# Layer 0's output projection in sixteen-tile block products, with on-chip shift columns, a ScalarE rotary exchange and another cut of the last two chunks

## The chip, the cores and the metric

One core of a Trainium2 chip runs the whole kernel. The metric is the time of one execution on the device in microseconds (us). The kernel before was timed three times: median 2083.02 us, from 2081.39 to 2084.38. A separate execution was taken with the profiler; every duration below is from that one.

## What is computed

A two-layer backbone works on 640 columns of activations: 128 context tokens and 512 latent tokens, 2048 features each. Cut to what matters here:

```
for l in (0, 1):
    h = rms_norm(x) * (1 + scale) + shift          # shift, scale, gate from silu(c) @ ada_w[l]
    q, k, v, ..., gp = split(h @ w_in[l])
    y = concat(branch_1, branch_2) * silu(gp)       # l = 0: window attention with rotary | GLA
                                                    # l = 1: neighbourhood attention | gMLP
    x = x + gate * (y @ w_out[l])                   # the output projection
out = rms_norm(x) * final_norm_g
```

The rotary embedding of layer 0 multiplies q and k by a cosine table and adds their 32-row blocks, exchanged in pairs (0 with 1, 2 with 3), times a sine table. Ten such steps run, for two k heads and eight q heads.

## The kernel before

All matrix products are fp32 in accuracy and are made of three TensorE products of two-part numbers: an activation is `acth + actl`, a weight is `whi + wlo`, and one product of a 128x128 weight tile costs three matmuls (high x high, high x low, low x high). Activations lie with features on the partitions, 16 k-tiles of 128 features, 640 columns in two halves of 320. `mm_k` and the inner function `three` of `spair` issue these matmuls (L396 is the helper `mm`).

**Weights.** A raw tile group of four k-tiles (128x512) is loaded from DRAM by SyncE, ScalarE copies it to `whi` (a rounding copy), and GpSimd or VectorE subtracts to `wlo`. `wpump` does this ahead of the matmuls, into a ring `whl` of 2560 columns, so at most five such units are live. The program is written by a planner in Python: it keeps a model of each engine's clock (class `Pace`), and tasks that yield (`spawn`, `tick`) issue their instructions between matmuls where that model says that there is room. Engines run their instructions in the order of issue, SyncE its DMAs too.

**Pairs of chunks.** An output chunk is 128 output features. Most chunks are computed two at a time as a 2x2 block product after Strassen and Winograd (`spair`): the blocks are the two chunks, the k-tiles 0 to 7 and 8 to 15, and the two column halves; seven block products stand in place of eight. Each product runs over four k-tiles per unit. The products named S1, S2 and A22 take sums of activations. For k-tiles 0 to 3 these sums stay on chip in `eh` and `el` (the near tiles); for k-tiles 4 to 7 (the far tiles) they lie in the DRAM tensor `far_dram` and are loaded to four slots of the pool `tail`, one load per slot and product, by `far_load`, each time after the product that last read the slot. S3 takes sums from `t3_dram`, which replace the second column half of `acth` and `actl` for k-tiles 0 to 7 while pairs run; `fold` makes all this, `unfold` brings the saved second half back from `bh_dram` and `bl_dram`. A pair can also be short (`ns == NR`): then only k-tiles 0 to 3 and 8 to 11 go through block products, the other eight are done plainly, and no far sums are needed. A full pair is 7 x 8 x 3 = 168 matmuls, a short one 7 x 4 x 3 + 2 x 8 x 2 x 3 = 180, two plain chunks 192.

**The output projections.** Each has 16 chunks: 0 and 1 as a plain pair (`kpair`), 2 to 13 as six pairs, 14 and 15 plain. `SHORT = 6, 2` says how many of the six are short: all six in layer 0, the first two in layer 1. In layer 0, chunks 14 and 15 are a `kpair` during which the next layer's activations are formed as tiles come free (`to_odd`: ScalarE writes `acth`, VectorE `actl`); while that runs, the shift columns of layer 1 (two columns per k-tile, `fs` for the far tiles) are computed and one DMA writes them to `far_dram`, whose rows have 2 + 320 columns. Then the plain pair of layer 1's first two chunks starts. VectorE also computes the adaLN vectors of the coming layers from `ada` rows in the background (custom instructions on `adas`).

**The last two chunks** (`hpair`, L955 on) end the program: half 0 of chunk 14, half 0 of chunk 15, then half 1 of each, so that the final norm of half 0 (`final(0)`) runs under half 1. Each half takes its own weight split: `unit(c, k, r)` for r = 0 and 1, sixteen units in all. After half 0, `prescale` multiplies five tiles (`POOLED`) of half 1 by the norm weight on ScalarE so that GpSimd can finish them. `final(1)` stands alone at the end: sum of squares, a product with ones, five steps to the reciprocal root, then a scaling of each of 16 tiles and 8 stores.

**Rotary** (`rope`): four DMAs of 32 rows each exchange the blocks of q within SBUF into `sw`, then VectorE multiplies and adds.

Of the kernel before, what the change touches and what calls it, by code (L numbers as in the profile page):

```python
# [32 lines left out]
NR = 4  # L33
CW = 2 + HT
RING = 2560
WINDOWS = ((0, 2), (2, 2), (4, 4), (8, 4))
# [7 lines left out]
GHOSTS = 12, 13  # L44
SHORT = 6, 2

# [189 lines left out]
class Trunk:  # L236
# [378 lines left out]
    def wstart(self, chunks, acts):  # L615
        self.chunks = chunks
        self.jobs, self.plain = [], []
        self.job, self.nraw, self.nsplit = 0, 0, 0
        self.parts, self.live, self.wpat = {}, {}, 0
        self.su, self.su_free = None, 0  # L620
        self.wfree_at = 0.0

        self.gates = []
        J = self.jobs

        def unit(c, k, r=0):
            gate, slot = self.gates.pop(0) if self.gates else (0, self.plain[-1][2] + 1 if self.plain else 0)
            J.append(("split", (c, k, r), slot % 4, 4, chunks[c][1]))
            self.plain.append((c, k, slot, gate))

        for k in (0, 4, 8, 12):
            for c in range(FIRST):
                unit(c, k)
        self.both = {c for kind, x in acts if kind == "h" for c in x[:2]}
        work = [x for x in acts if x[0] != "f"]
        for n, (kind, x) in enumerate(work):
            if kind == "c" and x >= FIRST:
                for k in (0, 4, 8, 12):
                    unit(x, k)
            elif kind == "k":  # L640
                seen = set()
                for c, k in self.skew(*x[:3]):
                    if (c, k - k % 4) not in seen:
                        seen.add((c, k - k % 4))
                        unit(c, k - k % 4)
            elif kind == "h":
                for r in range(2):
                    for c in x[:2]:
                        for k in (0, 4, 8, 12):
                            unit(c, k, r)  # L650
# [122 lines left out]
    def wpump(self, force=False):  # L773
# [47 lines left out]
        else:  # L821
            a = self.space(n * M)
            if a is None:
                return False
            hl = [x[:, a : a + n * M].rearrange("p (a b) -> p a b", b=M) for x in self.whl]
        outs = [] if lead else [pc.span(hl[0])]
# [5 lines left out]
        else:  # L832
            self.live[key] = (a, a + n * M)
            self.wpat = a + n * M
        hi, lo = hl
# [27 lines left out]
    def wdone(self, key):  # L863

        del self.parts[key]
        if key in self.live:
            del self.live[key]
        else:
            self.su_free += 1
# [12 lines left out]
    def mm_k(self, c, k, outs, first=0, last=KT - 1, r=0):  # L882
# [4 lines left out]
        for p, half in outs:  # L887
            cs = self.cols(half, shift)
            h, l = self.ah[:, k, cs], self.al[:, k, cs]
# [37 lines left out]
    def kpair(self, c1, c2, order, ready=None, free=None):  # L927
# [25 lines left out]
        self.quiet = False  # L953

    def hpair(self, c1, c2, after):  # L955

        for half in range(2):
            if half:
                self.need("unfold0", "unfold1")
                self.quiet, self.hold = True, 6.0  # L960
            for c in (c1, c2):
                if half == 0 and self.chunks[c][3]:
                    self.chunks[c][3]()
                p = self.pj()
                for k in range(KT):
                    self.mm_k(c, k, [(p, half)], r=half)
                    self.kdone(c, k, half)
                    if k % 2:
                        self.tick(1 + 2 * half)
                self.chunks[c][4](*((p, None) if half == 0 else (None, p)))  # L970
                self.drop(p)
# [217 lines left out]
    def fold(self, ready, used, far_used, shift=None, yt=None):  # L1189
# [59 lines left out]
        def shifts():  # L1249
# [4 lines left out]
            for f, x, scale in ((0, a, -1.0), (1, a, 1.0), (2, u, 1.0)):  # L1254
                self.split2(self.eh[:, :, f, 0:2], self.el[:, :, f, 0:2], x[:, :NR], scale)
                self.split2(fs[:, :, f, 0, :], fs[:, :, f, 1, :], x[:, NR:], scale)
                yield
            e = self.far.rearrange("p i f a b -> p (i f a) b")[:, :, 0:2]
            self.dma(e.bitcast(U32), self.fs.bitcast(U32))
            self.flags.add("shifts")  # L1260

        def far(w):
# [26 lines left out]
            for i in range(NR + w, NS, 2):  # L1289
                yield from self.wait(f"{ready}:{i}", f"{ready}:{NS + i}")  # L1290
                (j1, j2), (m1, m2) = [(x[:, one], x[:, two]) for x in (yt(i), yt(NS + i))]
                keep(i)
                out = lambda f: self.far[:, i - NR, f, :, 2:]
                yield from sub(j1, j2, j1)
# [844 lines left out]
    def out_evac(self, l, f, xsrc, spill):  # L2139
        nc = self.nc  # L2140
        box = {}
        at = HT

        def square(y, c):
            if l == 1 and f == KT - 1:
                nc.scalar.activation(self.sq, y[:, c], AF.Square)
            else:
# [190 lines left out]
    def program(self):  # L2338
# [5 lines left out]
        self.hsp = tc.nc.dram_tensor(HSP, [128, 6, T], F32, kind="Internal").ap()  # L2344
        self.far = tc.nc.dram_tensor(FAR, [128, NS - NR, 3, 2, CW], F32R, kind="Internal").ap()
        self.t3 = tc.nc.dram_tensor(T3D, [128, NS, 2, HT], F32R, kind="Internal").ap()
# [477 lines left out]
    def open_gate(self):  # L2824
# [3 lines left out]
        self.ssq, last = self.take(), self.take(1024)  # L2828
        self.last, self.sq = last, last[:, :HT]
        self.wsT, self.gb = (last[:, 512 * i : 512 * i + 512].rearrange("p (a b) -> p a b", b=128) for i in range(2))  # L2830
        L["ms"] = [self.xr.list[0][:, :HT], self.xr.list[1][:, :HT]]

    POOLED = (2, 5, 8, 11, 13)

    def prescale(self):
        c = slice(HT, T)
        for k in self.POOLED:
# [3 lines left out]
            yield  # L2841
        self.flags.add("prescaled")
        yield

    def final(self, half):
        nc, d, Y, L = self.nc, self.d, self.Y, self.L
        c = slice(HT, T) if half else slice(0, HT)
        n = c.stop - c.start
        x, t = (m[:, :n] for m in L["ms"])
        if half:  # L2850
            yield from self.wait("fr", "prescaled")
# [4 lines left out]
        yield from self.until(self.sq)  # L2856
        self.mm(p[:, :n], self.ones, self.sq, start=False)
        if not half:
# [4 lines left out]
        q = self.sm()[:, :n]  # L2863
        self.rsqrt(r, x, t, q)
        if half:
            nc.scalar.activation(r, q, AF.Copy)
            self.flush()
        else:
            self.flags.add("fr")
            self.spawn(self.prescale())  # L2870
            yield
        for k in range(KT):
# [3 lines left out]
            elif k % 2:  # L2876
                two = Y[:, k - 1 : k + 1, c]
            if half and k in self.POOLED:
                nc.gpsimd.tensor_tensor(y, y, r, ALU.mult)
# [184 lines left out]
```

## Time and profile before

| | |
|---|---|
| median of three runs | 2083.02 us (2081.39 to 2084.38) |
| the profiled execution's own time | 2079.31 us |
| its span, first to last instruction | 2077.5 us |
| TensorE busy | 2026.5 us, 98% |
| VectorE, GpSimd, ScalarE busy | 73%, 53%, 46% |
| mean granted TensorE clock | 0.994 of full speed |
| moved by DMA | 412.52 MB, mean 199 GB/s |

How to read it: matmuls overlap, so a matmul's own duration (some 310 ns) is longer than the step from one to the next, and a busy TensorE says only that something was in its pipe. The stages lie in the span as follows, by the loads of their weights: layer 0's output projection from about 845 to 1050 us, layer 1's from about 1850 to the end, the last two chunks from 2027.6 us.

### The profile page before, as it was taken

Reading aid. Unit: us, or ns where it says so; the run is one execution under the profiler, and the core shown is the slowest. Engines: PE = TensorE matmul, PEld = TensorE weight load, DVE = VectorE, ACT = ScalarE, POOL = GpSimd, SP = SyncE. Lnnn points to the kernel's source line nnn. Section 1 sums busy time; section 2 is a strip of 40 time slices with the busy share of each in tenths; the row PEclk is TensorE's granted clock in tenths of the full one; section 3 lists DMA queues with packets and bytes.
Section 4 is the critical chain, followed back from the end, with each engine's and each line's share of the span. In section 5 each row is a group of like instructions: output and inputs, shape, how many; then the busy total and the mean of one; then the engine's idle time right before and its main releaser. Section 6 shows DMA issues by size and latency. Waiting matters only on the chain. (4 is left out here: it accounts for less than half of the span.)

```text
span 2077.5 us, 38922 instructions
## 1 busy us (share of the span) xinstructions
PE 2026.5 (98%) x13930; PEld 1965.5 (95%) x13930; DVE 1506.7 (73%) x3465; ACT 960.1 (46%) x1995; POOL 1095.4 (53%) x830
## 2 busy tenths in 40 slices
PE   7999999999999999999999999999999999999996
PEld 4888999999999999999989999999999999999996
DVE  1448788777878877688767778987785667676565
ACT  3345444452434454444554444455554544454443
POOL 3447333333232223476556675756666567658783
PEclk9999999999999999999999999999999999999998
DMA  9964333346454433777647856756655575567766
GB/s 374 337 218 139 124 115 129 122 137 192 149 163 143 137 118 121 253 248 223 187 147 260 271 192 234 246 198 213 223 194 194 180 255 194 184 223 243 248 198 217
DMA packets 215874, 412.52 MB, mean 199 GB/s; under 512 B 25664, under 2 KB 88320, under 8 KB 215680
## 3 DMA queue, kind: packets, MB, share of 16 engines
q1 hardware_dynamic: 214208, 408.43, 59.5%
q8 instruction: 109, 1.79, 0.4%
q10 hardware_dynamic: 1472, 1.61, 0.2%
q14 instruction: 85, 0.70, 0.1%
HBM read 368.88 MB, written 38.45 MB: 196 GB/s over the span
## 5 line engine op out<-in xcount | busy, mean ns | idle before, releaser
L396 PE MATMUL bank<-acth,whi 128*128 128x320 f32 (+1 forms) x3112 | 955.0, 318 | 12.0 <-DVE tail L210 4.2
L396 PE MATMUL bank<-acth,wlo 128*128 128x320 f32 (+1 forms) x3112 | 928.8, 310 | 3.2 <-POOL wlo L210 3.2
L396 PE MATMUL bank<-actl,whi 128*128 128x320 f32 (+1 forms) x3112 | 928.1, 310 | 0.0
L210 POOL TENSOR_TENSOR wlo<-wraw,whi 128x512 fp32r<-128x512 f32 x363 | 507.0, 1403 | 668.4 <-ACT whi L210 595.6
L396 PEld LDWEIGHTS bank<-acth,whi 128*128 128x128 f32 x3112 | 578.3, 189 | 23.5 <-issue 10.3
L396 PEld LDWEIGHTS bank<-acth,wlo 128*128 128x128 f32 x3112 | 578.0, 189 | 4.5 <-POOL wlo L210 4.5
L396 PEld LDWEIGHTS bank<-actl,whi 128*128 128x128 f32 x3112 | 578.4, 189 | 1.7
L210 POOL TENSOR_TENSOR wlo<-rs,whi 128x512 fp32r<-128x512 f32 x292 | 404.9, 1399 | 188.6 <-ACT whi L210 159.9
L210 ACT ACTIVATE whi<-wraw 128x512 fp32r<-128x512 f32 x393 | 240.4, 624 | 165.8 <-PE bank L396 107.0
L210 ACT ACTIVATE whi<-rs 128x512 fp32r<-128x512 f32 x329 | 201.3, 625 | 103.1 <-PE bank L396 60.7
L210 DVE CUSTOM_DVE_ANT_0 adas<-adas,bank,partg 128x256 bf16<-128x256 f32 (+1 forms) x320 | 178.0, 556 | 19.0 <-DMA adas<-ada_g 9.6
L396 PE MATMUL bank<-tail,whi 128*128 128x322 f32 (+1 forms) x672 | 152.0, 313 | 0.0
L210 ACT ACTIVATE arena<-arena,bc 128x128 f32<-128x128 f32 (+3 forms) x167 | 83.5, 519 | 142.5 <-DVE bc L210 96.5
L396 PE MATMUL bank<-eh,whi 128*128 128x322 f32 (+1 forms) x444 | 138.8, 313 | 0.0
L396 PE MATMUL bank<-el,whi 128*128 128x322 f32 (+1 forms) x444 | 137.8, 310 | 0.0
L396 PE MATMUL bank<-eh,wlo 128*128 128x322 f32 (+1 forms) x444 | 137.7, 310 | 0.0
L210 DVE TENSOR_TENSOR bank<-bank,sums 128x320 f32<-128x320 f32 (+1 forms) x162 | 76.6, 494 | 66.8 <-PE bank L396 59.3
L210 ACT ACTIVATE Y<-bank 128x128 f32<-128x128 f32 (+5 forms) x134 | 52.1, 411 | 135.9 <-PE bank L396 70.1
L210 ACT ACTIVATE sums<-bank 128x320 f32<-128x320 f32 (+1 forms) x125 | 54.4, 435 | 128.0 <-PE bank L396 121.1
L396 PEld LDWEIGHTS bank<-tail,whi 128*128 128x128 f32 x672 | 112.2, 189 | 0.2
L210 DVE TENSOR_TENSOR rs<-rs 128x512 f32<-128x512 f32 x83 | 85.2, 1033 | 31.2 <-POOL wlo L210 30.8
L396 PE MATMUL bank<-tail,wlo 128*128 128x322 f32 (+1 forms) x336 | 103.9, 309 | 0.0
(227 smaller groups left out, 2872.2 us busy)
## 6 DMA issues: line engine op xcount, KB each, us to landing
tail<-far_dram SPq DMA_DIRECT2D x196, 322.0 KB, 4.3
wraw<-w_even SPq DMA_DIRECT2D x176, 256.0 KB, 3.2
adas<-ada_g SPq DMA_DIRECT2D x128, 256.0 KB, 3.8
adas<-ada SPq DMA_DIRECT2D x128, 256.0 KB, 3.7
rs<-w_odd SPq DMA_DIRECT2D x63, 512.0 KB, 5.4
wraw<-w_odd SPq DMA_DIRECT2D x37, 512.0 KB, 5.3
more<-ada SPq DMA_DIRECT2D x36, 512.0 KB, 7.2
rs<-w_out SPq DMA_DIRECT2D x30, 512.0 KB, 5.7
```

The source lines that it names most:

```text
L210: return f(*args, **kw)
L396: self.nc.tensor.matmul(out, lhsT, rhs, start=start, stop=stop, **kw)
```

## The change

Four things are edited.

1. `SHORT` goes from `6, 2` to `2, 2`, and layer 0's `fold` gets a name for its far tiles (`"us0"`), so that it makes far sums as layer 1's does.
2. The shift columns of the far tiles are no longer written to DRAM. Rows of `far_dram` have 320 columns now, and each `far_load` of a pair that needs shift columns is preceded by a GpSimd copy of two columns by two rows from `fs` into the slot.
3. `rope` exchanges the blocks with four ScalarE copies of 32 partitions by 512 columns instead of four DMAs.
4. `hpair` takes its columns as 384 and 256 (`CUT`), goes through the k-tiles of both chunks alternately in the first part (k 8 to 15 of each, then 0 to 7 of each), and splits each weight once: the units of k 8 to 15 stay in the ring, those of k 0 to 7 are parked in `eh` and `el`. The sum of squares, `prescale` (now for both parts) and `final` follow that cut, and `POOLED` is 3, 5, 7, 11, 13.

```
-SHORT = 6, 2
+SHORT = 2, 2
+CUT = 384
...
+            if key[0] in self.both and key[1] < NS:
+                a = 0
+                i = 2 * (key[0] != min(self.both)) + key[1] // 4
+                hl = [x[:, i].rearrange("p f c -> p (f c)")[:, : n * M] for x in (self.eh, self.el)]
...
+        return [(c, k) for a in (NS, 0) for c in (c1, c2) for k in range(a, a + NS)]
...
-        for half in range(2):
+        self.spawn(self.prescale(0))
+        steps = self.halves(c1, c2)
+        first, last = steps[0][1], steps[-1][1]
+        for half, cs in enumerate((slice(2, 2 + CUT), slice(2 + CUT, 2 + T))):
             if half:
-                self.need("unfold0", "unfold1")
+                steps.sort(key=lambda x: x[0])
...
+                if half == 0 and k < self.deep:
+                    self.need(f"unfold{k // 4}")
+                self.mm_k(c, k, [(banks[c], cs)], first, last)
...
-        o = 0 if shift else 2
-        self.dma(self.slots[i][:, :, o:].bitcast(U32), self.far[:, i, f, :, o:].bitcast(U32))
+        if shift:
+            x = self.fs[:, 6 * i + 2 * f : 6 * i + 2 * f + 2, :]
+            self.nc.gpsimd.tensor_copy(self.slots[i][:, :, 0:2], x)
+        self.dma(self.slots[i][:, :, 2:].bitcast(U32), self.far[:, i, f].bitcast(U32))
...
-            e = self.far.rearrange("p i f a b -> p (i f a) b")[:, :, 0:2]
-            self.dma(e.bitcast(U32), self.fs.bitcast(U32))
...
+        yield from self.clear("a", [sw], [q[:, s]])
         for i, j in ((0, 1), (1, 0), (2, 3), (3, 2)):
-            self.dma(sw[32 * i : 32 * i + 32, :], q[32 * j : 32 * j + 32, s])
+            self.nc.scalar.activation(sw[32 * i : 32 * i + 32, :], q[32 * j : 32 * j + 32, s], AF.Copy)
...
-        do(lambda: self.fold("y0", "uo0", None))
+        do(lambda: self.fold("y0", "uo0", "us0"))
...
-    POOLED = (2, 5, 8, 11, 13)
+    POOLED = (3, 5, 7, 11, 13)
...
-            self.spawn(self.prescale())
+            self.spawn(self.prescale(1))
```

Since the planner writes the program, the edits also move instructions elsewhere. Three places follow. Numbers behind names are the tiles' own; "x" counts equal instructions in a row.

SyncE's queue before, at the passage from layer 0 to layer 1, while chunks 14 and 15 of layer 0 are computed (`x1T_dram` keeps the new x, `fs` are the shift columns, `w_odd` the weights of layer 1):

```order
L434 DMA x1T_dram<-arena_7767 128x640
L434 DMA tail_81<-x1T_dram 128x640
L434 DMA arena_7767<-xT 128x640 x2
L434 DMA far_dram<-fs_7762 3072x1x2
L434 DMA wraw<-w_odd 128x512 x7
L434 DMA x1T_dram<-tail_81 128x640
```

The same place now:

```order
L435 DMA acth<-bh_dram 128x320
L435 DMA actl<-bl_dram 128x320
L435 DMA arena_7775<-xT 128x640 x2
L435 DMA wraw<-w_odd 128x512 x7
L435 DMA x1T_dram<-tail_10059 128x640 x2
```

The DMA of 3072 rows of two columns is gone from in front of the weights of layer 1, and the last two of eight `unfold` loads stand there now (before there were four, earlier).

ScalarE before, in the last two chunks of layer 1 (`adas` and `tail` rows are squares for the sum of squares of chunks 12 to 14):

```order
L210 ACTIVATE sums_7763<-bank_69 128x320
L210 ACTIVATE arena_7767<-adas 128x320 x2
L210 ACTIVATE whi<-wraw 128x512 x2
L210 ACTIVATE arena_7767<-tail_20285 128x320
L210 ACTIVATE whi<-wraw 128x512 x4
```

The same place now:

```order
L211 ACTIVATE sums_7771<-bank_69 128x320
L211 ACTIVATE arena_7775<-adas 128x320 x2
L211 ACTIVATE eh_7766<-wraw 128x512 x3
L211 ACTIVATE Y<-Y,small 128x384 x4
L211 ACTIVATE adas<-adas,small 128x384
L211 ACTIVATE arena_7775<-tail_20627 128x384 x2
L605 ACT_TABLE_LOAD
```

Before, weight copies stood behind the square of chunk 14 and went on through the second half; now the last weight copies stand ahead of the scalings and of the squares of chunks 14 and 15.

GpSimd before, in a full pair of layer 1 (`rs` and `wraw` hold raw weights):

```order
L210 TENSOR_TENSOR wlo<-rs_7760,whi 128x512 x10
L210 TENSOR_TENSOR wlo<-wraw,whi 128x512 x4
L210 TENSOR_TENSOR wlo<-rs_7760,whi 128x512 x8
L210 TENSOR_TENSOR wlo<-wraw,whi 128x512 x2
L210 TENSOR_TENSOR wlo<-rs_7760,whi 128x512 x2
```

GpSimd now, after as many low parts of layer 1:

```order
L211 TENSOR_TENSOR wlo<-wraw,whi 128x512 x4
L211 TENSOR_TENSOR wlo<-rs_7768,whi 128x512 x2
L211 COPY tail_11228<-fs_7770 128x2x2 x4
L211 TENSOR_TENSOR wlo<-rs_7768,whi 128x512 x6
L211 COPY tail_11228<-fs_7770 128x2x2 x2
```

Copies of the shift columns stand between the low parts of the weights now, four to a far product, 196 in all.

More of the change, by code (lines that the diff above doesn't have):

```diff
@@ L867, in wdone @@
             del self.live[key]
-        else:
+        elif key[0] not in self.both:
             self.su_free += 1
@@ L887, in mm_k @@
         for p, half in outs:
-            cs = self.cols(half, shift)
+            cs = half if isinstance(half, slice) else self.cols(half, shift)
             h, l = self.ah[:, k, cs], self.al[:, k, cs]
@@ L953, in kpair, with halves @@
         self.quiet = False
+    @staticmethod
+    def halves(c1, c2):
+        return [(c, k) for a in (NS, 0) for c in (c1, c2) for k in range(a, a + NS)]
     def hpair(self, c1, c2, after):
-        for half in range(2):
+        self.spawn(self.prescale(0))
+        steps = self.halves(c1, c2)
+        first, last = steps[0][1], steps[-1][1]
+        for half, cs in enumerate((slice(2, 2 + CUT), slice(2 + CUT, 2 + T))):
             if half:
-                self.need("unfold0", "unfold1")
+                steps.sort(key=lambda x: x[0])
                 self.quiet, self.hold = True, 6.0
[L961 to L971, printed above, removed]
+            banks = {}
+            for c, k in steps:
+                if c not in banks:
+                    banks[c] = self.pj()
+                    if half == 0 and self.chunks[c][3]:
+                        self.chunks[c][3]()
+                if half == 0 and k < self.deep:
+                    self.need(f"unfold{k // 4}")
+                self.mm_k(c, k, [(banks[c], cs)], first, last)
+                if half:
+                    self.kdone(c, k)
+                if half or k % 2:
+                    self.tick(1 + 2 * half)
+                if k == last:
+                    self.chunks[c][4](*((banks[c], None) if half == 0 else (None, banks[c])))
+                    self.drop(banks[c])
             self.spawn(after(half), first=True)
     def far_load(self, i, f, shift):
-        o = 0 if shift else 2
-        self.dma(self.slots[i][:, :, o:].bitcast(U32), self.far[:, i, f, :, o:].bitcast(U32))
+        if shift:
+            x = self.fs[:, 6 * i + 2 * f : 6 * i + 2 * f + 2, :]
+            self.nc.gpsimd.tensor_copy(self.slots[i][:, :, 0:2], x)
+        self.dma(self.slots[i][:, :, 2:].bitcast(U32), self.far[:, i, f].bitcast(U32))
     def spair(self, c1, c2, ns, used, back, end):
@@ L1292, in far @@
                 keep(i)
-                out = lambda f: self.far[:, i - NR, f, :, 2:]
+                out = lambda f: self.far[:, i - NR, f]
                 yield from sub(j1, j2, j1)
@@ L2141, in out_evac @@
         box = {}
-        at = HT
+        at = CUT if l and f in (KT - 2, KT - 1) else HT
         def square(y, c):
             if l == 1 and f == KT - 1:
-                nc.scalar.activation(self.sq, y[:, c], AF.Square)
+                nc.scalar.activation(self.sq[:, : c.stop - c.start], y[:, c], AF.Square)
             else:
@@ L2841, in prescale @@
             yield
-        self.flags.add("prescaled")
+        self.flags.add(f"prescaled{half}")
         yield
@@ L2846, in final @@
         nc, d, Y, L = self.nc, self.d, self.Y, self.L
-        c = slice(HT, T) if half else slice(0, HT)
+        c = slice(CUT, T) if half else slice(0, CUT)
         n = c.stop - c.start
@@ L2850, in final @@
         if half:
-            yield from self.wait("fr", "prescaled")
+            yield from self.wait("fr")
+        yield from self.wait(f"prescaled{half}")
         p = self.sm()
@@ L2877, in final @@
                 two = Y[:, k - 1 : k + 1, c]
-            if half and k in self.POOLED:
+            if k in self.POOLED:
                 nc.gpsimd.tensor_tensor(y, y, r, ALU.mult)
```

40 lines of the change are left out of this document (22 added, 18 removed).

## The prediction

> **What bounds the kernel now.** I read the page's busy shares first, then the chain that ended last, then who made TensorE (PE) wait, stretch by stretch.
>
> ```profile
> PE 2026.5 (98%) x13930; PEld 1965.5 (95%) x13930; DVE 1506.7 (73%) x3465; ACT 960.1 (46%) x1995; POOL 1095.4 (53%) x830
> 1849.34 96.47 PE bank L396 x653
> 1946.32 81.42 PE bank L396 x552
> ```
>
> PE is in use for 98% of the span, and in layer 1's output projection the chain is nothing but matmuls: 96.47 / 653 and 81.42 / 552 give 147.5 ns from one 320-column matmul to the next. So a matmul less is 0.1475 us less, wherever PE is fed without a gap. The waits of PE show where it is not. The rows are of the stretches 550 to 800 us, 1050 to 1075, 1075 to 1800, 1800 to 1850, 1850 to 2030 and 2030 to the end, the longest of each; from 845 to 1050 there is none at all.
>
> ```profile
> PE bank L396 <- DVE arena L210: 0.6, 1, 0.6
> PE bank L396 <- DVE tail L210: 4.0, 2, 3.3
> PE bank L401 <- ACT Y L210: 1.0, 2, 0.6
> PE bank L396 <- DVE arena L210: 1.6, 2, 1.2
> PE bank L396 <- ACT sums L210: 0.5, 1, 0.5
> PE bank L396 <- POOL wlo L210: 2.2, 2, 1.2
> ```
>
> Three things are to be had: matmuls; the 4.0 us at the passage to layer 1 (1050 to 1075); the 2.2 us in the last two chunks and the time after the last matmul.
>
> **1. Fewer matmuls.** Four pairs become full: 168 matmuls each in place of 180, 48 in all. PE did not wait in that stretch, so 48 x 0.1475 = 7.1 us go, if it is still fed.
>
> **2. What feeds the four pairs.** The far sums are new in layer 0. First rows: a VectorE weight sum in layer 0's projection, the same in layer 1's, a GpSimd far sum; then the DMA of layer 0's projection, of layer 1's, and of the start, where it is full.
>
> ```profile
> L210 DVE TENSOR_TENSOR rs<-rs 128x512 f32<-128x512 f32 x9 | 7.9, 876 | 0.6 <-POOL wlo L210 0.6
> L210 DVE TENSOR_TENSOR rs<-rs 128x512 f32<-128x512 f32 x13 | 15.9, 1236 | 12.9 <-POOL wlo L210 12.8
> L210 POOL TENSOR_TENSOR Y<-Y 128x320 f32<-128x320 f32 (+1 forms) x16 | 18.9, 1181 | 3.3 <-ACT Y L210 3.3
> 850.00:900.00 50.00, 50.00 (x342) 50.00 (x341) 36.60 (x85) 21.97 (x43) 31.36 (x25) 1.00 0.79 258
> 1850.00:1900.00 50.00, 50.00 (x341) 50.00 (x340) 34.51 (x51) 24.35 (x52) 41.68 (x36) 1.00 0.88 285
> 0.00:50.00 50.00, 35.72 (x268) 23.38 (x269) 10.06 (x26) 18.49 (x44) 17.38 (x20) 0.93 0.98 373
> ```
>
> GpSimd gets 32 far sums, 32 x 1.18 = 38 us, in some 80 us (it was busy 31.4 of 50; layer 1 runs at 41.7). VectorE gets 16 weight sums, 16 x 1.24 = 20 us, and the planner moves adaLN work past the stretch to make room. DMA gets 16 MB more (36 far loads and their stores and returns, less adaLN rows put off; counted from sizes), over some 190 us 84 GB/s on top of 258: about 340 where 373 is full. Layer 1's projection has the same work without adaLN, at 285 GB/s, and PE waited 0.5 us there. I take 1.0 us of cost; the ends are 0 and 8.6 (the second rival). A gain is excluded: there is no wait to remove.
>
> **3. The passage to layer 1.** One DMA of 24 KB in 8-byte rows (3072 of them) is removed from SyncE's queue. The first rows are DMA issues with KB and us to landing, around that place and over the whole run, then ScalarE (ACT) and PE in order of time, then two 4-us windows (PE and weight-load busy time, VectorE, ACT, GpSimd; granted clock; DMA).
>
> ```profile
> far_dram<-fs SPq DMA_DIRECT2D x1, 24.0 KB, 8.8
> wraw<-w_odd SPq DMA_DIRECT2D x4, 256.0 KB, 8.6
> wraw<-w_even SPq DMA_DIRECT2D x176, 256.0 KB, 3.2
> 1043.98 0.63 ACT L210 ACTIVATE whi<-wraw 128x512 fp32r<-128x512 f32 x1 [5.01 <-DMA wraw<-w_odd]
> 1053.87 1.00 PE L396 MATMUL bank<-acth,whi 128*128 128x322 f32 x2 [3.32 <-DVE tail L210]
> 1046.00:1050.00 4.00, 4.00 (x29) 4.00 (x29) 3.65 (x5) 3.97 (x8) 2.54 (x3) 1.00 0.40 127
> 1054.00:1058.00 4.00, 4.00 (x18) 3.86 (x18) 0.81 (x2) 2.33 (x5) 1.73 (x2) 0.63 0.67 246
> ```
>
> The tiny rows take 8.8 us to land and the layer-1 weights behind them 8.6 where others take 3.2. ACT stands 5.0 us for these weights, in front of the `acth` copies on which VectorE waits; VectorE then works off its backlog before it empties chunk 14's bank, and PE, out of banks, idles 3.3 us and 0.7 later. After that the granted clock falls: 18 matmuls in 4 us where 4 / 0.1475 = 27 fit, 9 x 0.1475 = 1.3 us. Together 4.0 + 1.3 = 5.3 us. With the DMA gone the weights land some 5.4 us earlier and ACT's wait goes; next in line is the chain ACT, VectorE, bank itself. The passage inside layer 1 (1800 to 1850), built alike and without tiny rows, cost 1.6 us. So I book 5.3 - 1.6 = 3.7; ends 0 (another wait holds ACT) and 5.3.
>
> **4. Shift columns by GpSimd copies.** 196 copies of four elements per partition, each waiting for the PE product that last read the slot. Behind them stand the low parts of the next weights (1.4 us each), and PE waits for those.
>
> ```profile
> L210 POOL TENSOR_SCALAR b<-small 128x32 f32<-128x32 f32 x1 | 0.3, 288 | 2.4 <-DMA small<-small 2.4
> L210 POOL TENSOR_TENSOR wlo<-wraw,whi 128x512 fp32r<-128x512 f32 x363 | 507.0, 1403 | 668.4 <-ACT whi L210 595.6
> ```
>
> 196 x 0.29 = 57 us of GpSimd at most, over 660 us in which it works 60%. It mostly waits for ACT (595.6 of 668.4), which waits for PE to free a ring slot; a copy asks for the same product, so it adds little to a wait that is there. PE waited for ACT, not for GpSimd, from 1075 to 1800 (the list above). I take 0.5 us; ends 0 and the first rival.
>
> **5. Rotary on ACT.** Four 64-KB DMAs of 2.0 us become four copies; the nearest ACT row has 512 columns on all partitions.
>
> ```profile
> arena<-arena SPq DMA_DIRECT2D x28, 64.0 KB, 2.0
> L210 ACT ACTIVATE whi<-wraw 128x512 fp32r<-128x512 f32 x393 | 240.4, 624 | 165.8 <-PE bank L396 107.0
> ```
>
> 40 x 0.62 = 25 us of ACT over 250 us. PE waited 0.6 us in 550 to 800, the cover being the chunks' own matmuls: nothing to win beyond 0.6, and if the cover were gone 2.5 us a head. I take 0.
>
> **6. The last two chunks.** Two gaps in PE's order of time, then the chain after the last matmul, then the stores after 2066 us.
>
> ```profile
> 2037.97 0.31 PE L396 MATMUL bank<-acth,wlo 128*128 128x320 f32 x1
> 2040.36 0.31 PE L396 MATMUL bank<-acth,whi 128*128 128x320 f32 x1
> ...
> 2054.96 0.31 PE L396 MATMUL bank<-acth,wlo 128*128 128x320 f32 x1
> 2057.34 0.31 PE L396 MATMUL bank<-acth,whi 128*128 128x320 f32 x1
> 2033.56 0.42 SPq L434 DMA_DIRECT2D actl<-bl_dram  x1
> 2060.62 0.55 DVE tail L210
> 2061.17 0.91 DVE adas L210 x2
> 2062.08 0.92 DVE tail L210 x2
> 2063.00 0.41 DVE arena L210
> ...
> 2066.55 0.55 DVE Y L210
> ...
> 2070.77 0.92 DVE tail L210 x2
> DMA packets 2176, 2.62 MB, mean 228 GB/s; under 512 B 128, under 2 KB 2176, under 8 KB 2176
> q1 hardware_dynamic: 1088, 1.31, 33.3%
> q10 hardware_dynamic: 1088, 1.31, 33.0%
> ```
>
> Each gap is four steps that should take 0.59 us and take 2.39 and 2.38: 3.6 us, both for weight splits of a half that had been split before. Eight units now do for sixteen, and ACT makes the last before the squares. So 3.6 goes; ends 0 and 3.6. What could be late next is `unfold`, needed in the first part now: chunk 14's k 7 comes after 48 + 21 matmuls of 384 columns, 69 x 0.177 = 12 us after 2027.6, and its last load was issued at 2033.56, 6 us before.
>
> 384 and 256 columns together cost what 320 twice do by any straight line (0.177 + 0.118); if 256 should not get shorter than 0.1475, 96 x 0.03 = 2.8 us come on top, so 0 to 2.8, and I take 0, since no row has a stream of 256. The Trainium skill (TensorE: Matmul & The Clock Gate, Back-to-back issue gap) gives N/2.4 + 2.5 ns, a straight line, and 26.1 us for either cut; the trace's 147.5 ns at 320 is above its 135.8.
>
> After the last matmul: four scalings of half 0 (1.83 us) stand before the norm step; they now come ahead of it, and about 1.0 of that is needed for the square and its sum anyway: 0.8. The emptying and the norm steps (0.55 + 3.55 us) have a fifth fewer columns: between 0 and 0.8, I take 0.5. The stores keep the DMA engines for 66.3% of 11.5 = 7.6 us; a fifth less is 1.5, the scalings before them 5.1 us, a fifth 1.0: I take 1.2. Together 2.5, ends 1.0 and 3.5.
>
> **The sum.** 7.1 + 3.7 + 3.6 + 2.5 = 16.9, less 1.0 + 0.5, is 15.4. The profiled execution took 2079.3 (its span 2077.5 and 1.8 around it), so 2063.9; the median of the runs is 3.7 above it, so **2067.6 us**.
>
> **Rivals.**
> *Copies hold GpSimd up (the slower side).* Place: layer 1's full pairs, 49 groups of four copies. Each makes GpSimd wait for PE inside a product; if its lead is used up, the next low part comes late. From 15.4 / 49 = 0.31 us a group the change gains nothing; at 0.9 us it is 44 us, 2111. For: the order puts low parts between copies. Against: GpSimd idles 40% there and PE never waited for it. 0.07.
> *Layer 0 is overfed.* If far loads land after 8.8 us, as behind the tiny rows, and not near 4, then of eight groups with leads of 3 to 7 units (12 x 0.1475 = 1.77 us each) one waits 8.8 - 5.3 and three 8.8 - 7.1: 8.6 us; or VectorE, with sums at 1.24 us and more beside GpSimd's 38 us, empties banks late, which I price alike. 2067.6 + 8.6 - 1.0 = 2075.2. For: 340 of 373 GB/s. Against: layer 1. 0.12. The Trainium skill (SBUF — State Buffer, Who interferes with whom) has a rule for it: a VectorE instruction with two SBUF inputs and a GpSimd one that reads SBUF shut each other out. By that rule the sums lengthen, and the trace agrees (0.88 to 1.24 us).
> *The passage stays* (ACT or VectorE held by something else): 2071.3. 0.10.
> *The last chunks don't gain*, the parked units being late by as much, since their place is free only after the last near product: 2071.2. 0.09.
>
> **How the numbers follow.** Forecast 0.62. Low end: all terms at their best, 7.1 + 5.3 + 3.6 + 3.5 = 19.5, and a run 1.5 off the median: 2062. High end 2077 takes in the second rival with the last or third added in part; beyond it are the first rival and a little more. 0.2% (4.2 us) is about what a measurement tells from no change; below 2078.8 lie the forecast, the third and fourth rival and most of the second: faster 0.88, same 0.06, slower 0.06.
>
> **What would show it.** Right: 48 matmuls fewer and still no PE wait in layer 0's projection; first `w_odd` loads landing in 3 to 4 us, PE's wait at the passage under 2 us and no clock drop there; one run of PE through the last two chunks; some 14 us, not 17, from last matmul to end. Wrong: PE waiting for `wlo` between GpSimd copies, for far loads in layer 0, or a passage as long as before.

## The result and the profile after

The changed kernel takes 2070.21 us, the median of five runs (2068.01 to 2073.32), against 2083.02 (2081.39 to 2084.38) for the kernel before: a ratio of 0.994, interval 0.9927 to 0.9954, 12.8 us less. The forecast was 2067.6, range 2062 to 2077.

The profiled execution is the first of the five, 2073.32 us (span 2071.5), and so the slowest of them, while the profiled one of before (2079.31) lay below all its timed runs. Between the two traces there are only 6.0 us; they show where time went, and the medians how much. The traces hold 13930 and 13882 matmuls, 48 apart as counted. So the same matmul can be looked up in both, and the difference of its two start times is a ledger. Positive is a loss, and in layer 0's pairs the 7.1 us of the 48 matmuls are taken out:

| stretch | forecast | trace |
|---|---|---|
| to the start of layer 0's pairs (845 us), with the rotary edit | 0 | -1.5 |
| 48 matmuls less | -7.1 | -7.1 |
| feeding layer 0's pairs (845 to 1038 us) | +1.0 | +10.1 |
| passage to layer 1 (1038 to 1089 us) | -3.7 | -2.6 |
| layer 1 up to its last two chunks, with the shift copies | +0.5 | +1.0 |
| last two chunks, to PE's last matmul, and the tail behind it | -3.6 and -2.5 | -3.5 and -2.4 |

The page says, as before, that PE is bound:

```profile
PE 2022.9 (98%) x13882; PEld 1958.4 (95%) x13882; DVE 1532.4 (74%) x3482; ACT 997.6 (48%) x2065; POOL 1182.0 (57%) x1061
```

**Layer 0's projection.** Four 50-us windows (busy time of PE, weight load, VectorE, ScalarE and GpSimd; the share of TensorE's full clock that was granted; DMA share and GB/s):

```profile
850.00:900.00 50.00, 49.29 (x335) 49.02 (x334) 37.00 (x71) 25.82 (x54) 43.38 (x39) 1.00 0.96 314
900.00:950.00 50.00, 46.51 (x296) 44.72 (x295) 43.02 (x88) 22.63 (x46) 36.92 (x30) 0.97 0.94 327
950.00:1000.00 50.00, 49.84 (x339) 49.57 (x338) 44.19 (x89) 23.59 (x48) 39.33 (x31) 1.00 0.89 305
1000.00:1050.00 50.00, 48.54 (x328) 47.96 (x327) 41.53 (x93) 31.86 (x79) 32.15 (x24) 1.00 0.74 246
```

Before, each of these windows held 341 or 342 matmuls; now the second holds 296, and the DMA engines are 94 to 96% busy in the first two. Of the 69 matmuls that the four windows are short, 46 are missing from the second. The first window holds no product on far tiles yet: the first far load is issued at 913.2 us and the first product on it starts at 922.96. So most of the loss lies where the first full pair begins, and in the third window, at a DMA share of 0.89, the full pairs run almost without a gap. How one gap comes about is read from ScalarE's and PE's order of time (start, length, what, idle time before it and what ended that):

```profile
913.85 0.63 ACT L211 ACTIVATE whi<-rs 128x512 fp32r<-128x512 f32 x1 [2.51 <-PE bank L397]
921.00 1.02 ACT L211 ACTIVATE Y<-Y,A 128x128 f32<-128x128 f32 x2 [6.52 <-DMA x1T_dram<-Y]
...
922.29 1.13 ACT L211 ACTIVATE whi<-wraw 128x512 fp32r<-128x512 f32 x2
```

```profile
922.96 0.56 PE L397 MATMUL bank<-tail,whi 128*128 128x320 f32 x2 [0.26 <-ACT whi L211]
...
924.60 0.41 PE L397 MATMUL bank<-tail,wlo 128*128 128x320 f32 x1 [1.08 <-POOL wlo L211]
...
935.98 0.41 PE L397 MATMUL bank<-acth,whi 128*128 128x320 f32 x1 [0.53 <-ACT sums L211]
...
944.30 0.77 PE L397 MATMUL bank<-tail,whi 128*128 128x320 f32 x2 [1.51 <-DMA tail<-far_dram]
```

ScalarE scales a tile of the new x in place and must wait until that tile is stored. The store stood behind three far loads and an adaLN row in SyncE's queue, and landed 5.8 us after its issue; ScalarE stood still 6.5 us with the next weight copies behind it, and PE waited 0.26 us for a high part and 1.08 us for a low part. At 944 us the far load itself is late.

**The passage.** ScalarE's wait there, before and after, then the same kind of window as shown of before:

```profile
ACT whi L210 <- DMA wraw<-w_odd: 5.0, 1, 5.0
```

```profile
ACT whi L211 <- DMA wraw<-w_odd: 1.3, 1, 1.3
```

```profile
1052.69 0.78 PE L397 MATMUL bank<-acth,whi 128*128 128x322 f32 x2 [0.65 <-DVE tail L211]
...
1072.77 0.56 PE L397 MATMUL bank<-acth,whi 128*128 128x322 f32 x2 [0.66 <-ACT whi L211]
...
1074.44 0.56 PE L397 MATMUL bank<-acth,wlo 128*128 128x322 f32 x2 [0.81 <-POOL wlo L211]
```

```profile
1054.00:1058.00 4.00, 4.00 (x29) 4.00 (x28) 0.04 (x1) 2.00 (x5) 2.26 (x3) 1.00 0.85 313
```

The wait of 3.3 us has become 0.65 and the clock stays whole; small waits for layer 1's next weights come later.

**The last chunks.** PE's waits from 2020 us on are one of 0.7 us, at the norm. The last product with weights ends at 2057.2 and the span at 2071.5, 14.3 us later.

```profile
PE bank L397 <- ACT arena L211: 0.7, 1, 0.7
```

```profile
2056.54 0.28 PE L397 MATMUL bank<-acth,el 128*128 128x256 f32 x1
2056.66 0.28 PE L397 MATMUL bank<-acth,eh 128*128 128x256 f32 x1
...
2056.90 0.28 PE L397 MATMUL bank<-acth,el 128*128 128x256 f32 x1
2057.01 0.59 PE L397 MATMUL bank<-arena,ones 128*128 128x256 f32 x2
```

### The profile page after: what moved, and what is told of

It reads as the page before. It is cut to its first block, busy times and chain, and to the rows that moved or that the text cites. A ratio compares the mean times of both kernels' runs of the same rounds, so it can differ in the third digit from the quotient of the medians.

```text
span 2071.5 us, 39158 instructions
## 1 busy us (share of the span) xinstructions
PE 2022.9 (98%) x13882; PEld 1958.4 (95%) x13882; DVE 1532.4 (74%) x3482; ACT 997.6 (48%) x2065; POOL 1182.0 (57%) x1061
## 5 line engine op out<-in xcount | busy, mean ns | idle before, releaser
L397 PE MATMUL bank<-acth,whi 128*128 128x322 f32 (+1 forms) x3016 | 924.6, 318 | 10.7 <-DVE arena L211 3.6
L397 PE MATMUL bank<-acth,wlo 128*128 128x322 f32 (+1 forms) x3016 | 899.5, 310 | 3.2 <-POOL wlo L211 2.9
L397 PE MATMUL bank<-actl,whi 128*128 128x322 f32 (+1 forms) x3016 | 897.9, 310 | 0.0
L211 POOL TENSOR_TENSOR wlo<-wraw,whi 128x512 fp32r<-128x512 f32 x350 | 489.9, 1407 | 595.1 <-ACT whi L211 550.2
L397 PEld LDWEIGHTS bank<-acth,whi 128*128 128x128 f32 x3016 | 559.8, 189 | 22.3 <-issue 6.7
L397 PEld LDWEIGHTS bank<-acth,wlo 128*128 128x128 f32 x3016 | 559.3, 189 | 6.1 <-POOL wlo L211 5.7
L397 PEld LDWEIGHTS bank<-actl,whi 128*128 128x128 f32 x3016 | 559.8, 189 | 1.8
L211 POOL TENSOR_TENSOR wlo<-rs,whi 128x512 fp32r<-128x512 f32 x301 | 424.1, 1421 | 136.7 <-ACT whi L211 124.6
L397 PE MATMUL bank<-tail,whi 128*128 128x322 f32 (+1 forms) x768 | 175.1, 315 | 2.3 <-DMA tail<-far_dram 1.9
L397 PEld LDWEIGHTS bank<-tail,whi 128*128 128x128 f32 x768 | 129.1, 190 | 4.0 <-DMA tail<-far_dram 2.6
```

Of the source, the lines that this page charges most:

```text
L211: return f(*args, **kw)
L397: self.nc.tensor.matmul(out, lhsT, rhs, start=start, stop=stop, **kw)
```

## The experiments

Ratios are to the kernel before on the same chip, with their 95% intervals; the medians of before were 2080.61, 2082.17 and 2079.73 us beside the three groups of four. The ledger of each run's trace (us against the trace of before; the matmuls saved are taken out of the second column):

| run | ratio (interval) | to 845 us | layer 0's pairs | passage | layer 1 | last chunks |
|---|---|---|---|---|---|---|
| changed kernel | 0.9940 (0.9927 to 0.9954) | -1.5 | +10.1 | -2.6 | +1.0 | -3.5 |
| edit 1 alone | 1.0043 (1.0029 to 1.0056) | -1.8 | +10.5 | +0.9 | +2.2 | -0.2 |
| edit 2 alone | 1.0008 (0.9999 to 1.0016) | +0.6 | 0 | -3.7 | +5.1 | +0.8 |
| edit 3 alone | 0.9989 (0.9980 to 0.9997) | -2.7 | 0 | -1.3 | +1.0 | +1.1 |
| edit 4 alone | 0.9969 (0.9959 to 0.9980) | 0 | 0 | -1.2 | +0.6 | -3.5 |
| edits 2, 3, 4 | 0.9936 (0.9924 to 0.9949) | -4.0 | 0 | -3.1 | +2.6 | -3.5 |
| later scalings | 0.9957 (0.9944 to 0.9969) | -2.7 | +9.2 | -0.1 | +2.2 | -3.5 |
| two full pairs | 0.9979 (0.9970 to 0.9988) | -4.5 | +4.6 | -2.6 | +7.2 | -2.8 |
| copies twice | 0.9980 (0.9971 to 0.9989) | -1.9 | +9.4 | -2.2 | +8.1 | -3.2 |
| no copies | 0.9952 (0.9939 to 0.9965) | -5.1 | +7.3 | -2.4 | +1.1 | -3.4 |
| no adaLN rows | 0.9937 (0.9924 to 0.9949) | -2.8 | +3.6 | -1.1 | +1.9 | -3.5 |
| wide rows | 0.9958 (0.9945 to 0.9970) | -2.8 | +8.0 | -1.8 | +2.6 | -3.5 |
| late copies | 0.9981 (0.9972 to 0.9990) | -2.5 | 0 | -3.1 | +9.5 | -3.5 |

One trace is one execution. Where kernels run the same code, cells still differ: the passage of edits 3 and 4 alone is 1.2 to 1.3 us from that of before, and the first column is -1.5 in the changed kernel and -5.1 in the run without copies, whose instructions and their order are the same up to there. So a cell is read with its neighbours.

**Edit 1 alone.**

```
-SHORT = 6, 2
+SHORT = 2, 2
-        do(lambda: self.fold("y0", "uo0", None))
+        do(lambda: self.fold("y0", "uo0", "us0"))
```

> The kernel before with edit 1 alone: layer 0's four pairs take full block products, the tiny-row DMA and all else stay. Theory of the prediction (48 matmuls less are 7.1 us, feeding them costs 1.0): ratio 0.9971, about 2076.9 us. Rival, from the ledger of the two traces (layer 0's projection gained 7.1 and lost 10.1 us to late weights, because SyncE stands before a far load, the store of the new x stands behind it, and ScalarE's scaling stands behind that store): 2083 to 2086 us, ratio 1.000 to 1.0015, with ScalarE waiting for x1T_dram stores for over 10 us between 840 and 1030 us.

It is slower by 0.43%, some 9 us, more than the rival gave. ScalarE waited 18.7 us for the `x1T_dram` stores between 840 and 1030 us, as the rival had it. Its profiled execution was the fastest of its five (2083.66 us, median 2088.86) and shows 10.5 us lost in layer 0's pairs. Where the median's further 5 us lie no trace shows, but the granted clock of the runs points to it: 0.995 in the profiled execution, 0.992 in the median one and 0.991 in the slowest (2092.77 us), and 0.003 of 2089 us is 6 us.

**Edit 2 alone.**

```
-        o = 0 if shift else 2
-        self.dma(self.slots[i][:, :, o:].bitcast(U32), self.far[:, i, f, :, o:].bitcast(U32))
+        if shift:
+            x = self.fs[:, 6 * i + 2 * f : 6 * i + 2 * f + 2, :]
+            self.nc.gpsimd.tensor_copy(self.slots[i][:, :, 0:2], x)
+        self.dma(self.slots[i][:, :, 2:].bitcast(U32), self.far[:, i, f].bitcast(U32))
...
-            self.dma(e.bitcast(U32), self.fs.bitcast(U32))
...
```

> The kernel before with edit 2 alone: no DMA of 3072 tiny rows at the passage to layer 1, shift columns copied by GpSimd in layer 1 (196 copies). Theory of the prediction (3.7 us less at the passage, 0.5 for the copies): 2079.8 us, ratio 0.9985; PE waits under 2 us at the passage. Rival (the passage gives 2.6 and the copies cost 1.0, as the ledger of the two traces has it): 2081.4 us, ratio 0.9992. Second rival (another wait holds ScalarE or VectorE at the passage): 2083 us or above, PE waiting 4 us as before.

No gain (1.0008). The trace splits it: the passage gives the 3.7 us that the forecast booked, and layer 1 takes 5.1 back. That these 5.1 are the copies' is not shown: 2.4 of them are lost before 1200 us, where PE waited 0.7 and 0.9 us for far loads and not for low parts, and with edit 3 alone, which has no copies, PE waited 1.6 us for a far load there.

**Edit 3 alone.**

```
...
-            self.dma(sw[32 * i : 32 * i + 32, :], q[32 * j : 32 * j + 32, s])
+            self.nc.scalar.activation(sw[32 * i : 32 * i + 32, :], q[32 * j : 32 * j + 32, s], AF.Copy)
...
```

> The kernel before with edit 3 alone: the rotary exchange by ScalarE copies in place of DMAs. Theory of the prediction (nothing to win but 0.6): 2083.0 us, ratio 1.000. Rival (the window stretch gained 2.0 us in the trace of the changed kernel, from 494 to 760 us, and this edit is the only one there): 2081 us, ratio 0.9990.

0.11% faster, 2.3 us, as the rival had it. VectorE's waits from 494 to 560 us, before and in this run, then PE's in the same order:

```profile
DVE Y L210 <- DMA arena<-Y: 5.0, 1, 5.0
DVE arena L210 <- DMA Y<-arena: 3.1, 1, 3.1
```

```profile
DVE Y L210 <- ACT arena L210: 1.8, 1, 1.8
```

```profile
PE bank L401 <- DVE arena L210: 1.7, 1, 1.7
PE bank L401 <- ACT arena L210: 1.4, 2, 1.0
```

```profile
PE bank L401 <- ACT arena L210: 0.4, 1, 0.4
```

VectorE stood 5.0 and 3.1 us for the first two exchanges and then had its queue to work off, and PE waited 3.1 us, 1.7 of them for VectorE and 1.4 for ScalarE. With ScalarE's copies (0.63 us each, by the trace) it waited 0.4. The other traces bear it out: from 494 to 550 us every kernel with this edit gains 2.2 to 3.8 us on the kernel before, and those without it lie between 0.8 us of gain and 1.7 us of loss.

**Edit 4 alone.**

```
-        for half in range(2):
...
-                    self.mm_k(c, k, [(p, half)], r=half)
...
+        for half, cs in enumerate((slice(2, 2 + CUT), slice(2 + CUT, 2 + T))):
...
+                self.mm_k(c, k, [(banks[c], cs)], first, last)
...
```

> The kernel before with edit 4 alone: last two chunks cut 384 and 256 with one split per weight. Theory of the prediction (gaps 3.6 and tail 2.5 us): 2076.9 us, ratio 0.9971, no PE gap over 1 us after 2027 us. Rival (the first part waits for the unfold loads, or the parked units come late): 2080 us or above, ratio above 0.9985.

0.31% faster, 6.4 us: the forecast's 6.1.

**Edits 2, 3 and 4, without 1.**

```
-SHORT = 2, 2
+SHORT = 6, 2
...
-        do(lambda: self.fold("y0", "uo0", "us0"))
+        do(lambda: self.fold("y0", "uo0", None))
```

> The changed kernel with edit 1 undone (edits 2, 3 and 4 stay): all six pairs of layer 0 short again. If edit 1 costs what it cost alone (8.9 us by its ratio of 1.0043), this kernel is the better one: ratio to before about 0.990. If edit 1 costs less in company, since the tiny rows no longer meet the far sums' traffic at the passage, ratio 0.994 to 0.997. By the prediction's term (edit 1 gains 6.1 us) it would be at 0.997.

0.9936 (0.9924 to 0.9949), against 0.9940 (0.9927 to 0.9954) with edit 1: by these intervals edit 1 brings nothing that can be told from zero.

**ScalarE's scalings 6 us later.**

```
                 yield from self.wait(f"sp{k}")
+                yield 6.0
                 yield from self.clear('a', [Y[:, k, :]])
```

> The changed kernel with one line more: ScalarE's scalings of layer 0's new x are issued 6 us later, so that they no longer stand waiting for the x1T_dram stores ahead of the weight copies. Theory (the loss in layer 0's projection is ScalarE held in order by stores that land late): ScalarE waits under 2 us for x1T_dram stores there (14.7 before), the loss of 10.1 us falls by 4 to 6, ratio to before 0.9915. Rival (the DMA engines are full, far loads and weights land late whatever ScalarE does): the loss stays at 8 to 10 us, ratio 0.994. Second rival (VectorE and GpSimd are overbooked): the same 0.994, with PE waiting for sums or wlo and no DMA row among the waits.

The first rival, as far as this goes. ScalarE's wait for the stores fell from 14.7 to 7.0 us, not to the 2 that were expected, and the loss only from 10.1 to 9.2. PE's waits from 840 to 1030 us, and three windows of this run:

```profile
PE bank L397 <- DMA tail<-far_dram: 2.3, 3, 1.6
PE bank L397 <- POOL wlo L211: 1.4, 3, 0.5
...
```

```profile
928.00:932.00 4.00, 2.08 (x13) 1.59 (x11) 0.69 (x1) 2.99 (x6) 2.06 (x2) 1.00 0.97 328
932.00:936.00 4.00, 2.93 (x10) 1.99 (x11) 0.34 (x1) 0.92 (x3) 1.32 (x2) 0.71 1.03 350
936.00:940.00 4.00, 4.00 (x16) 4.00 (x16) 3.83 (x11) 0.62 (x2) 2.15 (x2) 0.50 1.03 403
```

At the same place PE now waits for the far loads themselves, with the DMA engines full and, in the second window, VectorE, ScalarE and GpSimd mostly idle. So half of the wait for stores could go without the loss going.

**Two full pairs in layer 0.**

```
-SHORT = 2, 2
+SHORT = 4, 2
```

> The changed kernel with two full pairs in layer 0 in place of four: 24 matmuls (3.5 us) less than none, and half the far loads. If the loss goes with the far traffic: about 5 us lost, net loss 1.5 against none. If the loss is a threshold of the DMA engines, passed only by four pairs: under 2 us lost, ratio to before 0.993 or better.

Half the pairs, half the loss (4.6 us), as the far traffic would have it, but the trace puts it elsewhere. The longest wait of PE, 2.3 us at 930.8 us, comes before the first product on far tiles (974 us) and names VectorE's `sums`, which stood behind an adaLN step that had waited 0.74 us for its row. So this run gives a size and does not show that late far loads are the path. The whole kernel is slower than either neighbour, with 7.2 us lost in layer 1, where its code is theirs but laid out otherwise by the planner.

**Each copy twice.**

```
-            self.nc.gpsimd.tensor_copy(self.slots[i][:, :, 0:2], x)
+            for _ in range(2):
+                self.nc.gpsimd.tensor_copy(self.slots[i][:, :, 0:2], x)
```

> The changed kernel with each GpSimd copy of shift columns made twice: 392 copies for 196, the same result. Theory of the prediction (a copy costs little, 0.5 us for 196, since GpSimd waits there anyway): within 1 us of the changed kernel, ratio to before 0.994 to 0.9945. Rival (the copies hold GpSimd and the far loads up, and cost 2 to 6 us as the odd layer's ledger has it): 2 to 6 us more, ratio 0.995 to 0.997.

0.4% above the changed kernel, some 8 us, more than either expectation, and 7.1 us more in layer 1. The copies (group line: busy, mean ns, idle time before them) in the changed kernel, then here, then PE's two longest waits in layer 1 here:

```profile
L211 POOL CAST tail<-fs 128x4 fp32r<-128x4 f32 x196 | 51.6, 282 | 37.9 <-PE bank L397 35.9 <-DMA far_dram<-tail 0.4 <-DMA Y<-hT_dram 0.3
```

```profile
L211 POOL CAST tail<-fs 128x4 fp32r<-128x4 f32 x392 | 94.8, 257 | 31.0 <-PE bank L397 17.7 <-DMA far_dram<-tail 0.6
```

```profile
1214.87 0.42 PE L397 MATMUL bank<-acth,wlo 128*128 128x320 f32 x1 [1.57 <-POOL wlo L211]
...
1705.83 0.64 PE L397 MATMUL bank<-eh,wlo 128*128 128x322 f32 x1 [2.10 <-POOL wlo L211]
```

43 us more of GpSimd's time make low parts late: PE waited 4.1 us in all for them from 1075 to 1850 us, against 0.2 in the changed kernel. This is the slower-side rival's mechanism, and it sets in between one copy and two. Twice in layer 1 a lower granted clock came on top (0.61 from 1706 to 1710 us, 0.57 from 1852 to 1856).

**No copies.**

```
-            self.nc.gpsimd.tensor_copy(self.slots[i][:, :, 0:2], x)
+            self.pace.record("g", "tensor_copy", (self.slots[i][:, :, 0:2], x), {})
+            if self.slots[i].name + str(i) not in self.flags:
+                self.flags.add(self.slots[i].name + str(i))
+                self.nc.gpsimd.eng.tensor_copy(self.slots[i][:, :, 0:2], x)
```

> The changed kernel with the shift columns copied once per slot (8 copies) and not before each far load: 188 of the 196 copies are left out, so the two shift columns of the far products keep old values; the far loads stay 320 columns wide. In five traces with the copies PE lost 3 to 8 us from 1074 to 2023 us against the kernel before, in three without them 0.6 to 2.1. Theory (GpSimd held by the copies, 4.6 us): PE's loss there falls to about 1 us, ratio to before 0.992. Rival (320 columns make each far row two short pieces in place of one long one, and the loads land in 5.0 us, not 4.3): the loss stays at 3 us or more, ratio 0.994. By the prediction's term for the copies (0.5 us) nothing changes.

Layer 1 loses 1.1 us, as the theory had it (only 4 copies were left, one for each slot). The time does not show it: 0.9952, not the 0.992 of the theory, with an interval that overlaps that of the changed kernel. The profiled execution was the fastest of its five (2067.71 us, median 2071.36).

**No adaLN rows during layer 0's pairs.**

```
...
-            self.nc.sync.dma_start(out, in_)
+            real and self.nc.sync.dma_start(out, in_)
...
-                self.dma(todo[i][0](raws[i % 4]), todo[i][1])
+                self.dma(todo[i][0](raws[i % 4]), todo[i][1], not self.mute)
...
-        do(lambda: (self.need("ada_g0"), self.spawn(scales())))
+        do(lambda: (self.need("ada_g0"), self.spawn(scales()), setattr(self, "mute", True)))
...
```

> The changed kernel without the loads of adaLN and condition rows (some 40 of 256 KB) while layer 0's pairs run; VectorE works on old rows, so the vectors are wrong, but each engine has the same instructions in the same order. Theory (the DMA engines are full there, 97 to 107% in the slices where PE waited): the loss in layer 0's projection falls from 9 to 10 us to under 4, ratio to before 0.990 to 0.991, far loads landing in under 5 us. Rival (ScalarE's, GpSimd's and VectorE's own work, or SyncE's order, holds the weights up): the loss stays at 8 us or more, ratio 0.994.

The theory's 3.6 us of loss, and 4.4 us less time than the two runs beside it on that chip (2066.88 against 2071.36 and 2071.25). Those two have no shift copies, and this one has them. The ratio of 0.9937 is above the 0.991 expected, and cannot be told from the changed kernel's 0.9940. PE's waits from 840 to 1045 us and two windows of this run, then the same windows of the run without copies:

```profile
PE bank L397 <- DMA tail<-far_dram: 1.0, 2, 0.9
PE bank L397 <- POOL wlo L211: 0.8, 2, 0.5
...
```

```profile
850.00:900.00 50.00, 50.00 (x342) 50.00 (x341) 40.92 (x81) 27.61 (x58) 46.24 (x42) 1.00 0.85 281
900.00:950.00 50.00, 48.46 (x327) 47.68 (x326) 42.77 (x83) 23.61 (x46) 38.53 (x30) 1.00 0.77 255
```

```profile
850.00:900.00 50.00, 50.00 (x342) 50.00 (x341) 40.31 (x83) 25.47 (x54) 45.46 (x42) 1.00 0.97 323
900.00:950.00 50.00, 47.16 (x312) 45.57 (x312) 42.51 (x81) 22.51 (x45) 37.38 (x29) 1.00 0.96 339
```

VectorE and GpSimd do what they did and are about as busy or busier in these windows. The first window proves nothing: it is full at a DMA share of 0.85 here and at 0.97 there. The second does: 327 matmuls at 0.77, against 312 at 0.96 and the changed kernel's 296. But the rows' loads leave three things at once, the DMA engines, SyncE's queue and VectorE's waits for rows, and which of them counts the run cannot say.

**Wide far rows, no copies.**

```
-            self.nc.gpsimd.tensor_copy(self.slots[i][:, :, 0:2], x)
-        self.dma(self.slots[i][:, :, 2:].bitcast(U32), self.far[:, i, f].bitcast(U32))
+            self.pace.record("g", "tensor_copy", (self.slots[i][:, :, 0:2], x), {})
+        o = 0 if shift else 2
+        self.dma(self.slots[i][:, :, o:].bitcast(U32), self.far[:, i, f, :, o:].bitcast(U32))
...
```

> As the run without copies, but the rows of the far tensor have 322 columns again and the far loads of layer 1 take them whole, with fixed values in the two shift columns that one early DMA of tiny rows writes in the window stretch; no copies at all. If the short pieces cost something: far loads land in about 4.3 us, as before, and not 5.0, and PE's loss from 1074 to 2023 us is 1 us or less, 2 us below the run without copies. If not: the same as that run. The early DMA may cost up to 3 us in its own place, before 845 us, which is left out of this comparison.

The far loads of layer 1 landed in 4.7 us (median), between the 4.3 of the kernel before and the 4.9 of the run without copies, and layer 1 lost 2.6 us, not less than that run's 1.1. No gain from wide rows shows.

**Late copies, on edits 2, 3 and 4.**

```
...
-            self.nc.gpsimd.tensor_copy(self.slots[i][:, :, 0:2], x)
...
+            y = self.slots[i][:, :, 0:2]
+            s, at = [pc.span(y), pc.span(x)], pc.ready("g", [pc.span(self.slots[i])], [])
         self.dma(self.slots[i][:, :, 2:].bitcast(U32), self.far[:, i, f].bitcast(U32))
+        if shift:
+            pc.late.append((lambda: self.nc.gpsimd.tensor_copy(y, x), s, lambda: at))
...
```

> Edits 2, 3 and 4 without edit 1, each copy of shift columns issued only when the planner takes PE's product on that slot for done, so that GpSimd does not stand waiting in front of the low parts; all results are computed. If the copies cost by waiting in order: 2 to 4 us less than the same kernel with early copies (0.9936), ratio 0.992. If they cost by their own 0.2 us each, or nothing: 0.9936.

Slower, 0.9981, and no test of the question. VectorE's low parts from `rs` over the whole run, in the same kernel with early copies and here:

```profile
L211 DVE TENSOR_TENSOR wlo<-rs,whi 128x512 fp32r<-128x512 f32 x36 | 40.9, 1139 | 18.4 <-ACT whi L211 18.2
```

```profile
L211 DVE TENSOR_TENSOR wlo<-rs,whi 128x512 fp32r<-128x512 f32 x123 | 97.8, 808 | 26.7 <-ACT whi L211 22.7 <-DMA far_dram<-tail 3.4
```

The planner's model took GpSimd for busy and gave low parts to VectorE instead (123 of these for 36), for which PE then waited 4.4 us in all. Nor did the copies stop standing in front of PE's products: GpSimd waited 48.8 us for them here. Whether the copies cost mainly by their own 0.28 us or by GpSimd standing in front of PE's product (35.9 us in the changed kernel) stays open.

## Why the prediction was right, and where it was not

The total was 2.6 us too low and the direction right. Partly that is luck: the term for feeding layer 0 was some 8 us too small, and the step from one execution to the median of the runs, taken as fixed, made up for most of it.

1. *Fewer matmuls*: 48, as counted. (The first of the two quotients for the step is 147.7 ns, not 147.5, which on 48 matmuls is 0.01 us.)
2. *Feeding layer 0* is the step that failed most: 1.0 us was booked, and six traces with four full pairs and their adaLN rows lost 7.3 to 10.5, near the 8.6 of the second rival, which had a chance of 0.12. The traffic was estimated well, if a little high (about 340 GB/s; 314 and 327 came). What failed is the step from there to a cost: "Layer 1's projection has the same work without adaLN, at 285 GB/s, and PE waited 0.5 us there." The 30 to 40 GB/s more were not free. Landings lengthened before the 373 GB/s was reached (last section), most of the loss fell at the start of the first full pair, and without the adaLN rows' loads 3.6 us are lost. So some 5.5 of the mean 9.1 hang on those loads, in one execution of that kernel; that the lengthened landings are the path is the likely reading and not shown, and the remaining 3.6 were not taken apart. The rival's VectorE part played little role. The Trainium skill (SBUF — State Buffer, Who interferes with whom) says that a VectorE instruction with two SBUF inputs contends with a GpSimd instruction that reads SBUF. The trace agrees: in the changed kernel the weight sums with no GpSimd instruction beside them took 0.69 us (22 of them), those with GpSimd busy nearly throughout 1.37 us (39). In layer 0's projection their mean rose from 876 to 1149 ns. Yet with the rows gone VectorE was as busy and PE waited less.
3. *The passage*: the DMA is gone, the clock drop too, and ScalarE's wait went from 5.0 to 1.3 us. The size is 3.7 in edit 2 alone and 2.6 in the changed kernel. There layer 0's last `unfold` loads stand just ahead of these weights, which land in 6.0 to 6.5 us, against 3.1 to 4.3 with edit 2 alone. In the run of edits 2, 3 and 4 they land in 4.7 to 5.9 us and the passage still gains 3.1.
4. *The copies*: the GpSimd time was right (51.6 us; 57 at most was forecast), their cover was not. With the copies layer 1 lost 1.0, 5.1, 2.6, 2.2, 7.2 and 1.9 us, mean 3.3; without them, before included, 0, 2.2, 1.0, 0.6, 1.1 and 2.6, mean 1.25. That is about 2 us where 0.5 was booked, with a spread as large as itself, and PE's waits there name far loads as well as low parts, so that all of it is the copies' is not shown.
5. *Rotary on ScalarE*: 0 was booked and 2.3 us came. The step "PE waited 0.6 us in 550 to 800" read the wrong window: the ten rotary steps begin at 494 us, and the 3.1 us that PE waited for them lie before 550.
6. *The last chunks*: gaps 3.5 (3.6 forecast), tail 2.4 (2.5). Matmuls of 384 and 256 columns step by 0.176 and 0.119 us, within 0.001 us of the straight line that was assumed (0.177 and 0.118), so that part cost nothing. `unfold` was in time.

By the ledgers the sum would have been some 8 us worse than forecast (feeding +8.1, passage +1.1, copies +1.5, rotary -2.3), and the two traces are 6.0 us apart where 15.4 was forecast, 9.4 worse. The medians show 2.6. The 6.8 us between are those of single executions from their medians, which the forecast took as a fixed 3.7 us: the profiled execution was 3.7 below its median for one kernel and 3.1 above for the other. No run says why, so this part of the agreement is luck.

What stays open: the four edits alone multiply to a ratio of 1.0009, and together they give 0.9940, 14 us apart. Edits 2, 3 and 4 alone multiply to 0.9966 and give 0.9936 together, which is 6 us of it. The other 8 are edit 1's, which costs 9 us alone and next to none in company. The traces account for 3.5 us of those at the passage, where edit 1 alone still meets the tiny rows (+0.9 against -2.6); for the rest there is no account; executions that were not traced, and the planner's new layout of layer 1 for each variant, may hold it. No version tried beat the changed kernel by more than its interval; the one without edit 1 equals it.

## What to carry to other kernels

Price added loads by the landing times of the loads around them, in the stretch where they are needed, and not by the transfer rate alone: here 50 us at a DMA share of 0.96 to 0.98 cost 1 us or nothing, where no far product ran, and the next 50 us, at 0.92 to 0.96, cost 4 to 7 us in every kernel with four full pairs and their adaLN rows. A cover is a stock: ask how much of it an edit uses up, and double the edit to see whether the next one still fits. A list of waits must begin where the edited step begins; a window that starts a little late can hide the whole gain.

## What the runs showed of the hardware

Landing times rose well before the 373 GB/s that this kernel's start holds over 50 us. From 850 to 950 us, adaLN rows of 256 KB before (254 GB/s in the mean) and after (321 GB/s):

```profile
adas<-ada SPq DMA_DIRECT2D x34, 256.0 KB, 4.6
```

```profile
adas<-ada SPq DMA_DIRECT2D x22, 256.0 KB, 6.5
```

And a short wait of PE can be followed by a lower granted clock that costs as much again. In the changed kernel a wait of 1.51 us ends at 944.30; the window from 944 us on has a granted clock of 0.57 and 14 matmuls where 27 fit, which is 13 x 0.1475 = 1.9 us, 0.3 of it the end of the wait:

```profile
940.00:944.00 4.00, 2.68 (x17) 2.15 (x15) 3.64 (x7) 1.86 (x4) 2.55 (x2) 1.00 1.06 390
944.00:948.00 4.00, 3.70 (x14) 3.48 (x15) 4.00 (x8) 0.68 (x2) 2.69 (x2) 0.57 0.99 382
```

The wait of 1.57 us at 1214.87 in the run with doubled copies had no such drop. Nor does the length of the wait tell which it will be. At the passage inside layer 1 PE waits 1.29 us at the same place of the program in eight of the kernels: at 1845.9 us in the changed kernel, where the 4 us from 1848 on have the whole clock and 25 matmuls, and at 1846.9 us with edit 2 alone, where they have a clock of 0.68 and 21 matmuls. It fell in four of the eight; the ledger puts it at 0.9 us each time.
